# One hybrid decoder layer in fp32: the order and pacing of background weight sums, and the order of seven Strassen products

## The chip, the cores and the metric

The kernel runs on one core of one Trainium2 chip. The metric is the time of the whole program on the device, in microseconds; before the change it is 2766.74, the median of three runs from 2760.09 to 2771.63. The core has five engines that run side by side and wait for each other through semaphores: TensorE (PE in the profile) multiplies matrices into PSUM, VectorE (DVE) and ScalarE (ACT) do elementwise work, GpSimd (POOL) does elementwise work and issues some transfers, SyncE (SP) issues most of them. Transfers run on 16 DMA engines that all queues share.

## The reference, cut to what matters

One layer of a decoder is computed for 2048 prompt tokens and 64 sample tokens (8 sequences of 8), all in fp32:

```python
h = rms_norm(x, norm_mix_pre[l])
proj = h @ w_in                                   # 1024 x 3080
q, k, v, z, xbc, dt_raw, b_gate, c_gate, u_c = split(proj)
# A: three dilated attention branches, merged;  B: Mamba-2 scan;  C: gated short convolution
out = concatenate([o_a, y_b, y_c], axis=-1) @ w_out
x = x + rms_norm(out, norm_mix_post[l])
h = rms_norm(x, norm_mlp_pre[l])
f = square(relu(h @ w_mlp_up[l])) @ w_mlp_down[l]  # 1024 x 4096, 4096 x 1024
x = x + rms_norm(f, norm_mlp_post[l])
```

Keys, values and recurrent states are outputs too, so the projections store K and V as they are made.

## The kernel before, in words

**Products.** Every large fp32 product is three products of split parts: an operand is a rounded part `hi` (ScalarE) and a rest `lo` (VectorE or GpSimd), and `mm3` adds hi x lo, hi x hi and lo x hi in one PSUM bank. So each weight tile is loaded (`wraw`), split into `whi` and `wlo`, and used.

**The first part** (`front`) goes over four blocks of 512 prompt tokens. `in_qkv(B)` makes K, V and Q of a block and stores them: K and Q in the three layouts of the branches, K and V rows to the outputs as well, through the tiles `kt` and `vt`, which share three buffers with the tag `s1`. `in_rest(B)` makes everything else of the block (convolutions, scan, gates). The order is `in_qkv(b0)`, `in_rest(b0)`, then `in_qkv` of b3, b2 and b1 in a row, then `in_rest` of b1, b2, b3. The normalised and transposed input of b3 and of b2 is written to memory after it is built (`spill`, 16 transfers of 256 KB a block) and read back for `in_rest`. Attention and scan run beside this as streams. Then comes the output projection (`out_proj`), with the attention of the sample tokens as a stream, then the MLP.

**The MLP** goes over three blocks of 704 tokens. Each of its two products is a Strassen product in Winograd's form: seven products of half size instead of eight. The seven are numbered; `UP_ORDER` and `DOWN_ORDER` say in which order they run. Each is eight steps (`steps`); `w_load` loads the weights of the step four ahead, `w_split` splits the next. The left operands of the second product are formed from the tiles `x[1,1]`, `x[1,2]`, `x[2,1]`, `x[2,2]` in `down_form`; the results go to `y(t, d)` in `down_out`: token half t, column half d. In the second product the splits of weights run on VectorE, in the first on GpSimd. `end_tile` follows `down_out` with the sums of squares of finished quarters, and for products 5 and 6 two of the three token tiles are put off by a step (`late`). `next_block` loads and transposes the next block's inputs as a stream; its tiles share buffers with `x[2,2]`.

**The weight sums.** The products 5, 6, 7 and 4 take combinations of the four quarters of a weight matrix, w1 to w4 in `wsum` (product 5 takes w1, 6 takes w2, 7 takes w3, 4 takes w4). They are formed in memory by transfers alone, as a background task (`weight_sums`, kept in `behind`). A sum of a piece is a copy (kind "c") issued by SP and an accumulating transfer (kind "a") issued by GpSimd: w1 = b11 + b12 and w3 = b12 + b22 are made together in the kinds "c13" and "a13" (two transfers each), w2 = w1 + b22 in "c2" and "a2", w4 = w2 + b21 in "c4" and "a4". Each of the two matrices (u and d) is cut into 16 pieces, so there are 192 groups and 256 transfers of 256 KB. Each transfer is tied behind the last instruction of its engine with `issue_after`.

**What sets the order.** The program is written as generators. `TimedPE` counts matmul columns, 2400 a microsecond for split parts and a quarter of that for plain fp32, into `PE.us`. `poll` advances a stream when `PE.us` passes its due time, and takes the next group of sums when `behind[1]` is passed; each group moves that by `SUM_US`. If a group is still missing when `w_load` loads the first weight of a product that needs it, the loop there issues all groups up to it at once; `SUM_END` names the last kind that each product needs. The framework then orders each engine's instructions by this priority and its own estimate of when they are ready, allots buffers, and adds the semaphores.

The 192 groups are ordered by a loop over pieces in which each piece passes through the six kinds one round after the other, matrix u's pieces before d's:

```python
for s in range(len(at) + 5):
    for k, kind in enumerate(("c13", "a13", "c2", "a2", "c4", "a4")):
        if 0 <= s - k < len(at):
            group(kind, s - k)
```

Of the kernel before, what the change touches and what calls it, by code (L numbers as in the profile page):

```python
# [43 lines left out]
HT = 352  # L44
BT = 2 * HT
NSUM = 16
SUM_US = 6.4
SUM_END = {5: "a13", 7: "a13", 6: "a2", 4: "a4"}
NSP = 14

# [94 lines left out]
def hybrid_layer(ctx: ExitStack, tc: tile.TileContext, I, O, stage=9):  # L145
# [110 lines left out]
    def poll():  # L256
        for st in list(streams):
            if PE.us >= st[1]:
                advance(st)
        if behind and PE.us >= behind[1]:  # L260
            sums_on()

    behind = []
    formed = []

    def sums_on():
# [1006 lines left out]
    def weight_sums():  # L1273


        at = [(m, i) for m in "ud" for i in range(NSUM)]

        def transfer(eng, out, x, **kw):
            with tc.issue_after(eng.last):
                eng.dma_start(out, x, **kw)  # L1280

        def group(kind, piece):
            m, i = at[piece]
            n = wsum[m][0].shape[0] // NSUM
            r = slice(n * i, n * i + n)
            (b11, b12), (b21, b22) = corners[m]
            w1, w2, w3, w4 = wsum[m]
            out, src = {"c13": ((w1, w3), (b11, b12)), "a13": ((w1, w3), (b12, b22)), "c2": ((w2,), (w1,)),
                        "a2": ((w2,), (b22,)), "c4": ((w4,), (w2,)), "a4": ((w4,), (b21,))}[kind]
            for o, x in zip(out, src):  # L1290
                if kind[0] == "c":
                    transfer(SP, o[r], x[r])
                else:
                    transfer(G, o[r], x[r], accum_op=ALU.add)

        for s in range(len(at) + 5):
            for k, kind in enumerate(("c13", "a13", "c2", "a2", "c4", "a4")):
                if 0 <= s - k < len(at):
                    group(kind, s - k)
                    formed.append((kind, *at[s - k]))  # L1300
                    yield SUM_US

    corners = {}
    for m, w in (("u", I["w_mlp_up"][0]), ("d", I["w_mlp_down"][0])):
# [7 lines left out]
    def front():  # L1312
        rows = b0.prep()
        next(rows)
        next(rows)
        SP.dma_start(cst, I["c_main"])
        next(rows)
        load_gain(psT)
        next(rows)
        load_ahead(1)  # L1320
        next(rows)
        load_ahead(3)
        for _ in b0.build():
            pass
        load_vectors(psT)
        load_heads()
        SP.dma_start(abt, I["c_att"])
        load_prev()
        stream(side())
        behind.extend((weight_sums(), PE.us + 30.0))  # L1330
        yield from in_qkv(b0)
        negate_heads()
        stream(ssd_head(b0))
        def then(a, b, build=True):
            a.early = (lambda: stream(b.prep())) if build else (lambda: None)
            a.before_pair = lambda: stream(b.build() if build else b.reload())

        then(b0, b3)
        yield from in_rest(b0)
        b3.spill()  # L1340
        then(b3, b2)
        yield from in_qkv(b3)
        b2.spill()
        then(b2, b1)
        yield from in_qkv(b2)
        yield from in_qkv(b1)
        stream(ssd_head(b1))
        then(b1, b2, False)
        yield from in_rest(b1)
        stream(ssd_head(b2))  # L1350
        then(b2, b3, False)
        yield from in_rest(b2)
        stream(ssd_head(b3))
        b3.early = lambda: stream(transition())
        b3.before_pair = lambda: None
        yield from in_rest(b3)
# [209 lines left out]

    NJ = FF // P // 2
    TP = [(0, P), (P, P), (2 * P, HT - 2 * P)]
    UP_ORDER, DOWN_ORDER = (1, 2, 6, 7, 5, 3, 4), (1, 2, 7, 4, 5, 6, 3)
    e4 = s4 = w4 = r4 = v4 = f4 = y4 = t4 = psD = None  # L1570
    shifts = [(nm, src, b) for b in range(NB) for nm, src in (("s_k", "cache_attn_k"), ("s_v", "cache_attn_v"))]
    steps = [(kind, b, i, jj) for b in range(TT // BT) for kind, order in (("u", UP_ORDER), ("d", DOWN_ORDER))
# [214 lines left out]
    def down_out(i, p, ps):  # L1787
        n = TP[p][1]
        ps = ps[:n]

        def y(t, d, new=False):
            if new:
                Y[t, p] = y4.tile([P, D], F32, name=f"y{t}", tag="y")
            return Y[t, p][:n, 512 * (d - 1):512 * d]

        if i == 1:
            A.copy(y(1, 2, True), ps)
        elif i == 2:
            V.tensor_add(y(1, 1), ps, y(1, 2))
        elif i == 7:  # L1800
            V.tensor_add(y(2, 2, True), ps, y(1, 2))
        elif i == 4:
            V.tensor_add(y(2, 1), ps, y(2, 2))
        elif i == 5:
            for d in ((2, 2), (1, 2)):
                V.tensor_sub(y(*d), y(*d), ps)
        elif i == 6:
            for d in ((2, 1), (2, 2), (1, 2)):
                V.tensor_add(y(*d), ps, y(*d))
        else:  # L1810
            V.tensor_add(y(1, 2), ps, y(1, 2))
# [28 lines left out]

    def end_tile(i, p, ps):
        down_out(i, p, ps)
        for t, d in {2: [(1, 1)], 6: [(2, 1), (2, 2)]}.get(i, []):
            square(t, p, d)

    def half(b, t):
# [27 lines left out]
    for at, (kind, b, i, jj) in enumerate(steps):  # L1874
# [56 lines left out]
        if kind == "d":  # L1931
# [8 lines left out]
            if i == 3 and end:  # L1940
# [3 lines left out]
                for p in range(len(TP)):  # L1944
                    if last:
                        finish(p)
                    else:
                        late.append(lambda p=p, f=finish: f(p))
        if kind == "d" and i == 5 and jj == 4 and b + 1 < TT // BT:
            stream(next_block(b + 1))  # L1950
        if at % 20 == 10 and shifts:
            nm, sr, sb_ = shifts.pop(0)
# [42 lines left out]
```

## Time and profile before

| | |
|---|---|
| median of three runs | 2766.74 us |
| the profiled execution | 2772.1 us, its span 2770.3 us |
| TensorE busy | 2583.0 us, 93% of the span |
| VectorE, ScalarE, GpSimd busy | 1533.3, 1327.3, 1085.4 us |
| mean granted TensorE clock | 0.971 |
| moved by the DMA engines | 528.26 MB, mean 191 GB/s |

A row of the stage table gives the busy time of each engine in a stretch, the granted TensorE clock as a part of full speed, the mean busy share of the 16 DMA engines, and what they moved. A row of the waits names who waited for whom, how long in total, how often, and the longest. Line 137 is the helper through which the instructions of all engines but TensorE pass, so groups are told apart by the names of tiles. Weight loads (PEld) overlap with matmuls. In a row of one tile's instructions, the three times are the shortest, the median and the longest, in ns; then come the first and the last start.

### The profile page before, as it was taken

How to read it: one execution, taken by the hardware profiler on the slowest of the kernel's cores; microseconds unless marked ns; L12 is line 12 of the kernel's file. 1: busy time of each engine (PE TensorE's matmuls, PEld its weight loads, DVE VectorE, ACT ScalarE, POOL GpSimd, SP SyncE). 2: the span in 40 equal slices, each digit the busy share in tenths (PEclk: the TensorE clock that was granted, in tenths of full speed). 3: DMA queues.
4: the chain of work that ended last, by engine and by line, in shares of the span. 5: the costliest groups of instructions: out<-in, count | busy, mean ns of one | idle time of the engine just before them, and what ended most of it. 6: DMA issues, size and time to landing. Idle time of an engine off the chain costs nothing. (4 is left out here: it accounts for less than half of the span.)

```text
span 2770.3 us, 40697 instructions
## 1 busy us (share of the span) xinstructions
PE 2583.0 (93%) x14329; PEld 2183.1 (79%) x14329; DVE 1533.3 (55%) x2994; ACT 1327.3 (48%) x2776; POOL 1085.4 (39%) x1008
## 2 busy tenths in 40 slices
PE   7899888999999987999899999989999999999997
PEld 6898767877877865656799977779997779998775
DVE  4555536455466366555145456865446685454676
ACT  4444334435435433334455744545664455375444
POOL 4445435354354444334567500056620016661002
PEclk9999899999999988999999999999999999999999
DMA  7767998768677549878787555475434456543454
GB/s 211 210 175 221 276 245 246 199 186 225 188 205 208 156 126 290 263 234 281 210 244 207 172 162 171 139 216 169 167 129 152 135 165 205 172 167 119 130 156 95
DMA packets 426260, 528.26 MB, mean 191 GB/s; under 512 B 65482, under 2 KB 326130, under 8 KB 421448
## 3 DMA queue, kind: packets, MB, share of 16 engines
q1 hardware_dynamic: 411352, 483.45, 55.0%
q0 software_dynamic: 14704, 42.21, 9.3%
q8 instruction: 113, 1.85, 0.3%
q14 instruction: 91, 0.75, 0.1%
HBM read 447.90 MB, written 178.19 MB: 226 GB/s over the span
## 5 line engine op out<-in xcount | busy, mean ns | idle before, releaser
L137 POOL TENSOR_TENSOR wlo<-wraw,whi 128x512 fp32r<-128x512 f32 (+2 forms) x359 | 672.8, 1902 | 534.9 <-ACT whi L137 488.5
L137 ACT CAST whi<-wraw 128x1024 fp32r<-128x1024 f32 (+2 forms) x528 | 468.9, 892 | 410.0 <-PE pm L118 262.9
L118 PE MATMUL pm<-slo,whi 128*128 128x352 f32 x1344 | 437.3, 327 | 11.7 <-ACT whi L137 6.4
L118 PE MATMUL pm<-shi,wlo 128*128 128x352 f32 x1344 | 433.2, 328 | 6.9 <-POOL wlo L137 6.9
L118 PE MATMUL pm<-shi,whi 128*128 128x352 f32 x1344 | 438.7, 326 | 0.0
L118 PE MATMUL pm<-wlo,shi 128*128 128x512 f32 (+1 forms) x1008 | 398.3, 395 | 1.8 <-ACT shi L137 1.7
L118 PE MATMUL pm<-whi,shi 128*128 128x512 f32 (+1 forms) x1008 | 396.2, 393 | 0.0
L118 PE MATMUL pm<-whi,slo 128*128 128x512 f32 (+1 forms) x1008 | 336.5, 398 | 3.5 <-DVE slo L137 3.2
L137 DVE TENSOR_TENSOR wlo<-wraw,whi 128x1024 fp32r<-128x1024 f32 (+1 forms) x169 | 206.1, 1220 | 190.6 <-ACT whi L137 180.3
L118 PE MATMUL pj<-lo,whi 128*128 128x512 f32 (+1 forms) x720 | 274.8, 382 | 17.8 <-ACT xr L137 9.8
L118 PEld LDWEIGHTS pm<-slo,whi 128*128 128x128 f32 x1344 | 256.5, 191 | 14.5 <-ACT whi L137 7.7
L118 PE MATMUL pj<-hi,whi 128*128 128x512 f32 (+1 forms) x720 | 264.5, 367 | 0.0
L118 PE MATMUL pj<-hi,wlo 128*128 128x512 f32 (+1 forms) x720 | 263.8, 367 | 0.0
L118 PEld LDWEIGHTS pm<-shi,wlo 128*128 128x128 f32 x1344 | 254.9, 191 | 8.9 <-POOL wlo L137 8.8
L137 POOL TENSOR_TENSOR ssf<-ssf 128x1 f32<-128x1 f32 (+1 forms) x18 | 14.0, 775 | 627.1 <-ACT jkf L137 627.0
L118 PEld LDWEIGHTS pm<-shi,whi 128*128 128x128 f32 x1344 | 256.5, 191 | 0.2
L137 DVE TENSOR_TENSOR x<-pm,x 128x352 f32<-128x352 f32 x240 | 123.5, 521 | 227.9 <-PE pm L118 227.7
L118 PEld LDWEIGHTS pm<-wlo,shi 128*128 128x128 f32 (+1 forms) x1008 | 181.0, 180 | 60.8 <-ACT shi L137 11.0
L118 PEld LDWEIGHTS pm<-whi,slo 128*128 128x128 f32 (+1 forms) x1008 | 177.0, 179 | 61.0 <-DVE slo L137 14.3
L118 PEld LDWEIGHTS pm<-whi,shi 128*128 128x128 f32 (+1 forms) x1008 | 180.6, 179 | 49.6
L137 ACT CAST shi<-x 128x352 fp32r<-128x352 f32 x288 | 137.1, 484 | 158.7 <-DVE x L137 105.4
L137 ACT ACTIVATE x<-x 128x352 f32<-128x352 f32 x384 | 183.3, 495 | 43.9 <-DVE x L137 39.3
(322 smaller groups left out, 4744.6 us busy)
## 6 DMA issues: line engine op xcount, KB each, us to landing
wraw<-in_w_in SPq DMA_DIRECT2D x192, 256.0 KB
wraw<-u_d SPq DMA_DIRECT2D x96, 512.0 KB
wraw<-d_d SPq DMA_DIRECT2D x96, 512.0 KB
wraw<-in_w_mlp_up SPq DMA_DIRECT2D x72, 512.0 KB
wraw<-in_w_mlp_down SPq DMA_DIRECT2D x72, 512.0 KB
u_d<-in_w_mlp_up POOLq DMA_DIRECT2D x64, 256.0 KB, 5.8
d_d<-in_w_mlp_down POOLq DMA_DIRECT2D x64, 256.0 KB, 6.9
out_s_k<-in_cache_attn_k SPq DMA_DIRECT2D x8, 2040.0 KB
```

Of the source, the lines that this page charges most:

```text
L118: return self.eng.matmul(out, lhsT, rhs, **kw)
L137: out = f(*args, **kw)
```

## The change

The 192 groups take another order: matrix u before d, and in each the kinds "13", then "2", then "4", over all 16 pieces; the accumulate of a piece follows two pieces behind its copy. No group is issued while the three projections `in_qkv(b3)`, `in_qkv(b2)` and `in_qkv(b1)` are written out (`hold`); after them the due time is set to the present. The step between groups is 6.6 instead of 6.4.

In the second MLP product, the order of the seven products is 1, 2, 7, 5, 6, 4, 3 instead of 1, 2, 7, 4, 5, 6, 3. Product 5 first copies `y(2,2)` to `y(2,1)` on ScalarE, product 4 adds to `y(2,1)`, and the sum of squares of `y(2,1)` is taken after product 4. The stream of the next block starts at step 6 of product 6 (the fifth in the new order), where it started at step 4 of product 5 (the fifth in the old).

```diff
-SUM_US = 6.4
+SUM_US = 6.6
...
-        if behind and PE.us >= behind[1]:
+        if behind and not hold[0] and PE.us >= behind[1]:
             sums_on()
...
-        for s in range(len(at) + 5):
-            for k, kind in enumerate(("c13", "a13", "c2", "a2", "c4", "a4")):
-                if 0 <= s - k < len(at):
-                    group(kind, s - k)
-                    formed.append((kind, *at[s - k]))
-                    yield SUM_US
+        todo = [(k, p) for m in range(2) for w in ("13", "2", "4") for i in range(NSUM + 2)
+                for k, p in (("c" + w, i), ("a" + w, i - 2)) if 0 <= p < NSUM for p in [NSUM * m + p]]
+        for kind, piece in todo:
+            group(kind, piece)
+            formed.append((kind, *at[piece]))
+            yield SUM_US
...
+        hold[0] = True
         yield from in_qkv(b3)
         b2.spill()
         then(b2, b1)
         yield from in_qkv(b2)
         yield from in_qkv(b1)
+        hold[0] = False
+        behind[1] = PE.us
...
-    UP_ORDER, DOWN_ORDER = (1, 2, 6, 7, 5, 3, 4), (1, 2, 7, 4, 5, 6, 3)
+    UP_ORDER, DOWN_ORDER = (1, 2, 6, 7, 5, 3, 4), (1, 2, 7, 5, 6, 4, 3)
...
         elif i == 4:
-            V.tensor_add(y(2, 1), ps, y(2, 2))
+            V.tensor_add(y(2, 1), ps, y(2, 1))
         elif i == 5:
+            A.copy(y(2, 1), y(2, 2))
             for d in ((2, 2), (1, 2)):
                 V.tensor_sub(y(*d), y(*d), ps)
...
-        for t, d in {2: [(1, 1)], 6: [(2, 1), (2, 2)]}.get(i, []):
+        for t, d in {2: [(1, 1)], 6: [(2, 2)], 4: [(2, 1)]}.get(i, []):
             square(t, p, d)
...
-        if kind == "d" and i == 5 and jj == 4 and b + 1 < TT // BT:
+        if kind == "d" and i == 6 and jj == 6 and b + 1 < TT // BT:
             stream(next_block(b + 1))
```

More of the change, by code (lines that the diff above doesn't have):

```diff
@@ L259, in poll @@
                 advance(st)
-        if behind and PE.us >= behind[1]:
+        if behind and not hold[0] and PE.us >= behind[1]:
             sums_on()
     behind = []
+    hold = [False]
     formed = []
```

## The prediction

> **What bounds the kernel now.** I read the page first, then the busy times by stage, then, for the stage that stands out, the waits, the DMA queues and the transfers of the weight sums. The page says that TensorE sets the time, 93% busy over the whole span. What can be won is its remaining 187 us of idle time and the clock lost around it, so the question is where that lies.
>
> ```profile
> span 2770.3 us, 40697 instructions
> PE 2583.0 (93%) x14329; PEld 2183.1 (79%) x14329; DVE 1533.3 (55%) x2994; ACT 1327.3 (48%) x2776; POOL 1085.4 (39%) x1008
> ```
>
> The busy times by stage (columns: stretch in us, its length, busy time of each engine, granted clock, DMA share, GB/s). The rows are block 0's second projection part, the three pure attention projections (247 to 436), the other three second parts, the output projection, the first block's up product, its down product, and the next block's up product.
>
> ```profile
> 80.00:247.00 167.00, 156.06 (x1176) 148.79 (x1175) 98.37 (x239) 74.06 (x198) 82.88 (x99) 0.98 0.68 179
> 247.00:436.00 189.00, 160.27 (x914) 132.57 (x913) 80.88 (x171) 67.69 (x134) 87.48 (x94) 0.90 0.96 273
> 436.00:1036.00 600.00, 549.62 (x3235) 458.88 (x3233) 323.28 (x809) 266.82 (x724) 273.15 (x313) 0.96 0.68 189
> 1036.00:1306.00 270.00, 237.92 (x1273) 157.45 (x1274) 152.40 (x392) 103.35 (x298) 105.06 (x166) 0.94 0.88 269
> 1306.00:1576.00 270.00, 260.70 (x1526) 246.09 (x1525) 110.98 (x192) 153.05 (x288) 174.05 (x108) 0.98 0.73 216
> 1576.00:1820.00 244.00, 241.88 (x1062) 184.44 (x1061) 166.34 (x261) 122.48 (x207) 10.50 (x14) 1.00 0.51 161
> 1820.00:2046.00 226.00, 219.41 (x1344) 218.24 (x1343) 116.80 (x168) 135.12 (x235) 141.61 (x67) 0.98 0.51 163
> ```
>
> The projections at 247 to 436 have the highest DMA share (0.96) and the lowest clock (0.90); TensorE idles 189 - 160.3 = 28.7 us there. From 1306 on it idles little. The idle share runs with the DMA share: 8.4% at 0.68 (436 to 1036), 11.9% at 0.88, 15.2% at 0.96.
>
> Who ends those idle times (waits from 247 to 436: TensorE's rows, then ScalarE's), and the three instructions behind the longest:
>
> ```profile
> PE pk L118 <- DVE dtall L137: 14.7, 3, 8.5
> PE pj L118 <- DVE dtall L137: 6.2, 1, 6.2
> PE pkt L122 <- DVE yn L137: 4.1, 1, 4.1
> PE pkt L122 <- ACT kt L137: 3.3, 1, 3.3
> ...
> ACT kt L137 <- DMA out_p_k<-kt: 24.7, 5, 9.5
> ```
>
> ```profile
> 288.48 0.59 PE L118 MATMUL pk<-wlo,hi 128*128 128x264 f32 x1 [5.21 <-DVE dtall L137]
> ...
> 357.29 0.59 PE L118 MATMUL pk<-wlo,hi 128*128 128x264 f32 x1 [8.53 <-DVE dtall L137]
> ...
> 420.84 0.77 PE L118 MATMUL pj<-lo,whi 128*128 128x512 f32 x1 [6.20 <-DVE dtall L137]
> ```
>
> `kt` and `vt` share three buffers (tag s1). Each must be stored (`out_p_k`, `out_p_v`, `v_d`) before it is written again, and the PSUM bank of the V product stays full until `vt` and `dtall` have read it. So a late store holds ScalarE and VectorE, then TensorE. The stores are late because the DMA engines are full:
>
> ```profile
> q1 hardware_dynamic: 72935, 47.73, 84.3%
> q0 software_dynamic: 672, 3.67, 11.5%
> ...
> L137 POOL DMA_DIRECT2D u_d<-in_w_mlp_up x15: 757/822/1192, 251.4 to 434.2; - x15
> L137 SPq DMA_DIRECT2D u_d<-in_w_mlp_up x10: 504/542/586, 250.6 to 422.3; - x10
> L137 SPq DMA_DIRECT2D u_d<-u_d x6: 480/480/527, 286.0 to 427.2; - x6
> ```
>
> (Packets, MB, share of the 16 engines from 247 to 436; then the sums' transfers: count, issue time in ns, first and last start.) The 15 accumulates, 256 KB each, are nearly all of queue 0: 11.5% of 189 is 21.7 us, 1.45 us each. The 16 copies are 4.19 of queue 1's 47.73 MB; 4.19/47.73 of 84.3% of 189 is 14.0 us, 0.87 each. A mean transfer is 1.16 us of all 16 engines. Without them the stage's demand falls from 182 to 146 us (to 153 if only the 25 leave that the pacing counts below; the window's edges take in six of its neighbours').
>
> **What moves where.** The pacing clock counts matmul columns over 2400 a microsecond (fp32 four times), so where each group falls follows from the code alone. The three projections advance it by about 122, of which 93 are their own products (per block 4 tiles x 24 x 512 plus 96 x 264 columns): 19 groups, 25 transfers at a step of 6.4. These leave. With 122 more of delay, 192 steps of 0.2 more, and two transfers for each "13" group, the counts from before to after, worked out by stage: block 0's second part 33 to 42, the three other second parts 89 to 75, the output projection 62 to 76, the first up product 38 to 30, its down product 5 to 29. The total stays 256, and so do the matmuls and the bytes. The sums now end 160 later on that clock, at about step 40 of the first down product; the last eight groups aren't due when the first weight of product 4 is loaded (four steps ahead of step 40), so the loop in `w_load` issues them at once there.
>
> **The terms**, in us, minus for faster:
>
> 1. The three projections. Two readings. By the row of shares: 146 us of demand in some 172 is 0.85, where the stages around 0.88 idle 11.4%, so 28.7 falls to about 21, and the clock rises from 0.90 to about 0.945, 5% of 160: together -15. By the waits: the long stalls are 4.1 + 3.3 + 5.2, 8.5 and 0.9 + 6.2; the transfers issued from the start or the stall before up to each are
>
> ```profile
> L137 POOL DMA_DIRECT2D u_d<-in_w_mlp_up x4: 822/890/995, 251.4 to 285.2; - x4
> L137 SPq DMA_DIRECT2D u_d<-in_w_mlp_up x2: 505/546/586, 250.6 to 251.2; - x2
> L137 SPq DMA_DIRECT2D u_d<-u_d x1: 481/481/481, 286.0 to 286.0; - x1
> ...
> L137 POOL DMA_DIRECT2D u_d<-in_w_mlp_up x6: 772/875/1192, 303.5 to 346.5; - x6
> L137 SPq DMA_DIRECT2D u_d<-in_w_mlp_up x3: 504/536/585, 301.7 to 356.2; - x3
> L137 SPq DMA_DIRECT2D u_d<-u_d x2: 480/504/527, 303.0 to 337.4; - x2
> ```
>
> 8.4 us of engine time before the first and 13.0 before the second, so the first would keep 4 us and the other two vanish: -24, and -7 for the slow clock just behind them. I take -19, nearer to the first reading, because spills and loads of 256 and 512 KB fill the engines in bursts without any sum. Bounds -5 and -31.
>
> 2. Block 0's second part: 9 transfers more are 10 us, a share of 0.74; on the line from 0.68 to 0.88 that is 1.1% of 167: +2. Bounds 0 and +5.
>
> 3. The other second parts: 14 fewer, share down 0.03, 0.5% of 600: -3. Bounds -6 and 0.
>
> 4. The output projection: 14 more are 16 us, a share of 0.94; on the line from 0.88 to 0.96 it would idle 2.5% more of 270, +7, and +13 with the clock. But its idle time is ended by DMAs in few places:
>
> ```profile
> PE pt L122 <- DVE ct L137: 6.1, 1, 6.1
> PE pt L122 <- DVE clo L137: 6.0, 6, 2.3
> ...
> PE pkk L122 <- DMA kn<-in_cache_attn_k: 2.5, 3, 1.6
> PE pos L118 <- DMA vn<-in_cache_attn_v: 2.4, 4, 1.1
> ```
>
> I take +5. Bounds 0 and +13. The Trainium skill, DMA: Bandwidth & Descriptors, Issuing engines are not separate DMA queues, says that transfers from every issuing engine run on the same 16 DMA engines and interleave. Read strictly, this speaks against the change: work is moved, not removed, and a stage that is nearly full pays for all of it, so +16 here and a sum of -2. The rows of the two queues bear the sharing out (84.3% and 11.5% make the 0.96); whether the stage pays, they can't say.
>
> 5. The first block's MLP. The up product idles for other reasons: 0. In the down product 24 more transfers take the share from 0.51 to 0.62, on a POOL that is busy 10.5 of 244 us, and TensorE idles 2.1 us: +1, which holds the eight groups issued at once. Weight loads run four steps ahead (a step is 244/56 = 4.4 us). If the load of product 4 had to wait for the last of eight accumulates, cover is gone: +10, the upper bound; 0 the lower.
>
> 6. The order of the second product. Added: nine copies of 128x512 on ScalarE; the nearest row is the eviction in the same stage. VectorE's subtraction of `y(2,2)` waits for it, and behind that stand its next splits, which run a step ahead.
>
> ```profile
> L137 ACT COPY y<-pm 128x512 f32<-128x512 f32 (+1 forms) x3 | 1.8, 586 | 0.5 <-PE pm L118 0.4
> L137 DVE TENSOR_TENSOR y<-pm,y 128x512 f32<-128x512 f32 (+1 forms) x18 | 11.5, 682 | 1.3 <-PE pm L118 1.3
> ...
> L122 PE MATMUL pq<-cst,xt x36: 244/272/302, 1713.3 to 1751.3; 128*128 128x128 f32 x24, 96*128 96x96 f32 x12
> ...
> 1715.00:1820.00 105.00, 103.24 (x457) 77.59 (x456) 84.42 (x140) 56.10 (x98) 9.69 (x13) 1.00 0.59 191
> ```
>
> 9 x 0.586 = 5.3 us of ScalarE, busy half of the stage: hidden; 5.3 if not. Product 4's three additions and squares now stand right before product 3, undeferred. The next block's rows and transposes need the buffers of tile (2,2), which product 4 reads, so their end moves from 1751 to about 1785, 35 us before the next up product. VectorE is 80% busy in the last 105 us, and product 4 forms no difference on it (saving 16 x 0.52 = 8 us there), so this fits. +1 for two block changes; bounds -3 and +10.
>
> Sum: -19 + 2 - 3 + 5 + 1 + 1 = -13. The profiled execution took 2772.1 us (1.8 around its span), 5.4 over the runs' median of 2766.74. So 2759 there, **2754 as a median**.
>
> **Rivals.** (a) Full recovery: the stalls have no cause but the sums, and the later stages absorb them: -31 + 2 - 3 + 0 + 1 = -31, 2736. For it: 35 us of stall and lost clock in a stage whose demand falls by a fifth. Against: queue 1 keeps 146 us. (b) No recovery: three buffers and the bursts of spills make the stalls, sums or none; -5 + 2 - 3 + 5 + 2 = +1, 2768. For it, the slice of the first stall, whose share stands above 1 with only five of the sums issued since 250:
>
> ```profile
> 270.00:280.00 10.00, 5.06 (x36) 4.00 (x34) 1.63 (x3) 2.15 (x7) 4.38 (x9) 0.84 1.04 383
> ```
>
> (c) Slower: the accumulate catches up with its own copy. It was issued seven groups behind it (45 on the pacing clock), now three (20, some 22 us). POOL waits in order, and its splits of `wlo` for TensorE, norms and stores' inputs stand behind. What one such wait costs at the shortest distance is on record:
>
> ```profile
> POOL d_d L137 <- DMA d_d<-d_d: 20.2, 1, 20.2
> ...
> DMA to landing us min/median/max: 4.6/8.5/14.0
> ```
>
> The second row, the sums' accumulates in the output projection, shows landings up to 14 us from POOL's queue; the copies wait longer on SP's. If a third of the 66 accumulate groups before the MLP waited 3 us, POOL would lose 66 us, and with half of it past the four weight tiles of lead the price is +33: 2787. It decides from 27 us passed on. Against: the splits have slack, POOL is under half busy in every stage before the MLP.
>
> **How the numbers follow.** Forecast 0.46, own range 2742 to 2766; (a) 0.19, 2727 to 2742; (b) 0.17, 2762 to 2776; (c) 0.18, 2776 to 2800. A tenth left out on either side makes 2730 to 2784. About 0.5% is what a measurement of this kernel can tell from no change, that is 2753 and 2781. Faster: all of (a) and half of the forecast, 0.42. Slower: most of (c) and a little for term 4 at its bound, 0.19. Same: 0.39.
>
> **What would show it.** No `u_d` transfer between about 255 and the start of block 1's second part; the share of these projections near 0.85, their idle time near 15 us, the clock at 0.94 or more; ScalarE's wait for `out_p_k` under 12 us. The output projection at a share of 0.94 and at most 5 us longer. The last `d_d` accumulates near 1735, all at once, with no idle time of TensorE behind them; the up products' starts unmoved against their down products. It is wrong if the projections keep their stalls with the sums gone (b), if POOL waits for `u_d` copies by tens of us (c), or if the output projection grows by ten.

## The result and the profile after

The changed kernel takes 2747.44 us (median of five runs, 2745.07 to 2754.54) where the kernel before takes 2766.74 (median of five, 2760.09 to 2771.63). The ratio is 0.9925, with a 95% interval from 0.9908 to 0.9942: faster by 0.75%, and by more than 0.5% over the whole interval. The forecast was 2754, so the gain is 19 us where 13 were predicted.

The first two lines of the page after:

```profile
span 2752.8 us, 40740 instructions
PE 2578.7 (94%) x14329; PEld 2179.7 (79%) x14329; DVE 1510.2 (55%) x2994; ACT 1332.3 (48%) x2785; POOL 1086.8 (39%) x1008
```

This profiled execution is the longest of the five runs (2754.54 us), as the profiled one of before also lay 5 us over its median; their spans differ by 17.5 us.

The prediction's stage table used round times. To compare two kernels, each stage has to begin and end at the same instruction, so the rows below are cut at marks found in each trace: the first three rows are block 0's second part, the three pure projections (from the last eviction of the second K of block 3 to the last Q eviction of block 1) and the other second parts up to the first product with `w_out`; then the output projection, the same together with the first up product, and the first down product. The busy times by stage of before, between these marks (stretch in us, length, busy times, granted clock, DMA share, GB/s):

```profile
77.40:267.70 190.30, 179.23 (x1321) 169.38 (x1320) 108.67 (x255) 85.65 (x223) 95.67 (x114) 0.98 0.71 192
267.70:435.00 167.30, 138.71 (x784) 113.80 (x784) 71.93 (x153) 55.89 (x111) 76.87 (x80) 0.89 0.96 272
435.00:1002.20 567.20, 520.21 (x3110) 437.10 (x3109) 310.36 (x786) 256.10 (x696) 263.16 (x300) 0.96 0.70 194
1002.20:1345.50 343.30, 307.16 (x1579) 206.91 (x1579) 182.68 (x453) 130.37 (x372) 135.84 (x204) 0.94 0.79 241
1002.20:1576.30 574.10, 529.33 (x2930) 426.40 (x2931) 277.46 (x612) 268.38 (x615) 289.40 (x287) 0.96 0.78 234
1576.30:1819.60 243.30, 241.18 (x1057) 183.76 (x1056) 165.64 (x260) 121.78 (x206) 10.50 (x14) 1.00 0.51 161
```

The same rows of the changed kernel:

```profile
78.30:270.90 192.60, 182.66 (x1332) 171.96 (x1331) 110.11 (x255) 85.71 (x223) 98.76 (x117) 0.97 0.77 210
270.90:420.70 149.80, 135.13 (x786) 111.92 (x786) 68.94 (x148) 55.94 (x112) 67.81 (x68) 0.94 0.89 254
420.70:989.60 568.90, 524.15 (x3109) 441.88 (x3107) 310.44 (x792) 255.93 (x696) 258.88 (x296) 0.95 0.68 187
989.60:1328.70 339.10, 305.02 (x1580) 205.00 (x1579) 169.82 (x453) 130.36 (x372) 138.99 (x210) 0.94 0.85 256
989.60:1557.90 568.30, 524.23 (x2931) 422.31 (x2930) 265.27 (x612) 268.68 (x614) 288.89 (x288) 0.96 0.79 240
1557.90:1803.00 245.10, 242.02 (x1058) 183.84 (x1057) 165.59 (x260) 123.57 (x209) 20.66 (x26) 1.00 0.61 185
```

Stage by stage, after minus before: +2.3, **-17.5** in the projections, +1.7, -4.2 in the output projection, -1.6 in the up product (229.2 against 230.8, each the difference of two rows), +1.8 in the down product. What precedes 77.4 adds 0.9 and what follows the down product takes 0.9 off (949.8 against 950.7). The sum is the 17.5 by which the spans differ.

In the projections the DMA share fell from 0.96 to 0.89, the clock rose from 0.89 to 0.94, and TensorE's idle time fell from 167.3 - 138.7 = 28.6 to 149.8 - 135.1 = 14.7 us. The transfers of the up sums in a window that reaches some 20 us over the stage's start (250 to 421):

```profile
L137 POOL DMA_DIRECT2D u_d<-in_w_mlp_up x2: 857/943/1029, 251.2 to 251.8; - x2
L137 SPq DMA_DIRECT2D u_d<-in_w_mlp_up x2: 534/566/599, 403.5 to 405.2; - x2
L137 SPq DMA_DIRECT2D u_d<-u_d x1: 510/510/510, 385.8 to 385.8; - x1
```

None is issued between 252 and 385. The last three start ahead of the stage's end, although the program writes their groups behind the third projection; they are plain copies on SP's queue. The waits of TensorE, and the wait of ScalarE for its stores, in the same stretch:

```profile
PE pk L118 <- DVE dtall L137: 11.2, 2, 6.7
...
ACT kt L137 <- DMA out_p_k<-kt: 17.9, 5, 5.3
```

Of the three long stalls of before two are left, with 11.2 us in place of 14.7 + 6.2, and the wait for `out_p_k` fell only from 24.7 to 17.9. So the wait is the one that the prediction named, but it does not go away with the sums.

In the first down product, GpSimd's wait and one of its rows in order of time (start, duration, what ended the idle time before it), then TensorE's waits:

```profile
POOL d_d L137 <- DMA d_d<-d_d: 154.5, 11, 16.9
```

```profile
1714.98 2.50 POOL L137 DMA_DIRECT2D d_d<-in_w_mlp_down  x3 [12.62 <-DMA d_d<-d_d]
```

```profile
PE pm L118 <- ACT shi L137: 1.1, 3, 0.6
PE pm L118 <- DVE wlo L137: 1.1, 1, 1.1
PE pq L122 <- DMA xt<-xn_d: 0.5, 1, 0.5
```

GpSimd stood 154.5 of 245 us before accumulates, the last three of which were issued together at 1715. TensorE waited 2.7 us in all, for other things. The next block's transposes in the same product:

```profile
L122 PE MATMUL pq<-cst,xt x36: 246/271/302, 1732.2 to 1763.1; 128*128 128x128 f32 x24, 96*128 96x96 f32 x12
```

They end 205 us into the product where they ended 175 into it (1751.3 - 1576.3), 40 us ahead of the next up product at 1803.

### The profile page after: what moved, and what is told of

Same layout as the page of the kernel before. It is cut to its first block, busy times and chain, and to the rows that moved or that the text cites. A ratio compares the mean times of both kernels' runs of the same rounds, so it can differ in the third digit from the quotient of the medians.

```text
span 2752.8 us, 40740 instructions
## 1 busy us (share of the span) xinstructions
PE 2578.7 (94%) x14329; PEld 2179.7 (79%) x14329; DVE 1510.2 (55%) x2994; ACT 1332.3 (48%) x2785; POOL 1086.8 (39%) x1008
## 5 line engine op out<-in xcount | busy, mean ns | idle before, releaser
L118 PEld LDWEIGHTS pm<-whi,slo 128*128 128x128 f32 (+1 forms) x1008 | 178.3, 179 | 62.1 <-DVE slo L137 12.5
```

What stands on the lines that cost most here:

```text
L118: return self.eng.matmul(out, lhsT, rhs, **kw)
```

## The experiments

The theory was the prediction's: the sums keep the DMA engines full in the projections, three buffers pass that on to TensorE, and the pause takes it away; what the sums then cost elsewhere goes with the DMA share of the stage. The rivals: the stalls come from the spills and the short ring of buffers, sums or none (b); they come from the sums alone (a); or the gain is owed to another part of the change, the new order of the groups or of the products. Ratios are to the kernel before in runs on the same chip.

### One part alone, and no sums at all

Three kernels each have one part less or one part alone. The changed kernel without the pause:

```diff
-        hold[0] = True
         yield from in_qkv(b3)
...
-        hold[0] = False
-        behind[1] = PE.us
```

> The changed kernel without the pause: new order of the sums, step 6.6, new product order. Theory (the pause frees the DMA engines in the three pure projections): the projections take some 165 us again instead of 150, and the whole is within 0.4% of the kernel before (2757 to 2772). Rival (the order of the sums or of the products makes the gain): at least two thirds of it stay, 2747 to 2754, with the projections still near 167.

The kernel before with these three lines (and the test of `hold` in `poll`), with its old order of groups, its step of 6.4 and its old order of products:

> The kernel before with the pause alone: old order of sums and of products, step 6.4. By the code's own clock two groups are then missing when product 7 of the first down product is loaded and eleven when product 4 is, and they are issued at once. Theory: the projections still shrink by 14 to 18 us; if the groups issued at once cost nothing, the whole gains 12 to 18 (2749 to 2755); if the weight loads wait for them, TensorE idles up to 15 us in the first down product and the whole gains 0 to 8. Rival (order makes the gain): projections unchanged.

The kernel before with the new order of the products alone:

```diff
-    UP_ORDER, DOWN_ORDER = (1, 2, 6, 7, 5, 3, 4), (1, 2, 7, 4, 5, 6, 3)
+    UP_ORDER, DOWN_ORDER = (1, 2, 6, 7, 5, 3, 4), (1, 2, 7, 5, 6, 4, 3)
...
+            A.copy(y(2, 1), y(2, 2))
```

> The kernel before with the new order of the second product alone. Theory: each down product 1 to 2 us longer, each up product of blocks 2 and 3 up to 3 us shorter, the whole within 5 us of before (2762 to 2772), no change in the projections. Rival (the product order makes part of the gain): 2755 or less.

And the kernel before without any transfer of the sums; the four products that used them read as many bytes of plain quarters of the weights, so the MLP's result is of other weights:

```diff
-                    5: wsum[m][0], 6: wsum[m][1], 7: wsum[m][2], 4: wsum[m][3]} for m in "ud"}
+                    5: corners[m][0][0], 6: corners[m][1][0], 7: corners[m][1][1], 4: corners[m][0][1]} for m in "ud"}
...
-        behind.extend((weight_sums(), PE.us + 30.0))
```

> The kernel before with no weight sums at all: the four products that take them read plain quarters of the weights instead, so the second half of the layer is computed from other weights; every product, split and load of a weight stays, 256 transfers go. It bounds what any pacing of the sums can win. Theory: the projections shrink by 15 to 20, the rest of the first part and the output projection by 15 to 30 together, the MLP by under 3: 2715 to 2738. If only the projections are hurt by sums, 2745 to 2752.

Measured:

| kernel | median us | ratio to before, interval |
|---|---|---|
| before, on this chip | 2769.88 | 1 |
| change without the pause | 2776.54 | 1.0033, 1.0021 to 1.0044 |
| pause alone | 2763.68 | 0.9980, 0.9966 to 0.9993 |
| new order of products alone | 2771.29 | 0.9995, 0.9979 to 1.0010 |
| no sums | 2705.54 | 0.9772, 0.9755 to 0.9788 |

The stage rows of the kernel without the pause (the projections, the output projection):

```profile
268.90:443.70 174.80, 138.24 (x786) 113.99 (x786) 65.95 (x152) 56.12 (x112) 77.42 (x83) 0.87 0.93 257
...
1003.70:1357.00 353.30, 309.60 (x1581) 207.59 (x1580) 175.64 (x453) 130.62 (x372) 137.98 (x206) 0.93 0.78 240
```

Those of the pause alone:

```profile
264.70:420.60 155.90, 135.64 (x786) 111.56 (x786) 69.16 (x151) 55.84 (x112) 67.99 (x68) 0.93 0.88 254
...
984.40:1330.80 346.40, 306.06 (x1580) 204.89 (x1579) 180.31 (x453) 129.99 (x372) 133.72 (x202) 0.95 0.77 238
```

Of the product order alone, the projections and the first down product:

```profile
264.30:428.00 163.70, 136.48 (x784) 112.39 (x783) 70.65 (x153) 55.61 (x112) 76.62 (x80) 0.91 0.97 276
...
1564.00:1809.40 245.40, 242.07 (x1057) 183.75 (x1056) 165.61 (x260) 123.50 (x209) 10.80 (x14) 1.00 0.50 160
```

And of the kernel without sums, the first five stages, then TensorE's longest wait in its projections:

```profile
76.30:258.50 182.20, 178.49 (x1332) 169.01 (x1331) 104.17 (x255) 86.31 (x224) 85.57 (x97) 0.99 0.55 158
258.50:408.20 149.70, 134.37 (x786) 111.37 (x785) 70.19 (x150) 55.92 (x112) 68.52 (x68) 0.94 0.86 247
408.20:951.10 542.90, 511.03 (x3108) 429.47 (x3107) 307.46 (x791) 255.99 (x697) 230.54 (x256) 0.97 0.56 161
951.10:1284.90 333.80, 305.19 (x1579) 205.75 (x1579) 178.95 (x451) 130.32 (x371) 107.78 (x171) 0.94 0.63 201
951.10:1510.80 559.70, 522.84 (x2930) 421.27 (x2930) 277.56 (x610) 268.87 (x613) 245.53 (x232) 0.97 0.60 192
```

```profile
PE pk L118 <- DVE dtall L137: 11.7, 2, 7.0
```

Three things follow. The projections take 149.7 us with no sums anywhere, and 149.8 in the changed kernel: the pause recovers all that the sums cost there, to within 3 us in later traces. And the 15 us of idle time that stay (149.7 - 134.4), with two waits for `dtall` of 11.7 us, need no sums. So (a) is refuted, since part of the stalls has another cause, and (b) is refuted as to its price. Second, the projections are long without the pause (164 to 175) and short with it (150 to 156), whatever the orders. Third, the pause alone wins only 0.20% in time, which its upper end leaves at 0.07%, and the change without the pause (new order and step of the groups, new order of the products) loses 0.33%: the 0.75% of the whole is not the sum of the two.

Three of these runs missed what was expected of them. The change without the pause was slower than its range (2776.54 for 2757 to 2772), and its projections longer (174.8 for some 165). The pause alone won 6 us where 12 to 18 were expected if the groups issued at once cost nothing; its first down product took 243.3 us, as before, so the rest is not lost there, and these traces don't show where it is. And the kernel without sums was faster than its range (2705.54 for 2715 to 2738): the second parts and the output projection gave 42 us instead of 15 to 30.

### The parts in pairs, the change again, and sums put later

The changed kernel once more, unaltered, on another chip:

> The changed kernel once more, beside its parts on one chip, for a second trace: 2744 to 2754, 0.7 to 0.8% below the kernel before. The projections at 150 us again if that is the place of the gain; more than 156 in this trace would say that the first trace flattered them.

The pause and the new order of the products, with the old order and step of the groups:

> The changed kernel with the old order of the sums and their old step: pause and new product order. By the code's own clock, two groups are issued at once for product 7 of the first down product, four for product 5 and the rest for 6 and 4 later. The pause alone gained only 0.2%. If its loss lay in groups issued at once under product 4, this gains most of the whole change: 2748 to 2756. If the order of the sums matters by itself beside the pause (fewer transfers in later parts), it stays at 2758 to 2766.

The changed kernel with the old order of the products:

> The changed kernel with the old order of the second product: pause and new order of the sums. 17 groups are missing when product 4 is loaded as the fourth and are issued at once. If weight loads wait for them, TensorE idles 5 to 20 us in the first down product: 2752 to 2768, and the new product order is there to prevent it. If they don't wait, it is as fast as the whole change or 3 to 5 us faster (no copies on ScalarE, no longer down products): 2742 to 2750.

And the changed kernel with a wider step for matrix u and a narrow one for d, so that more of the sums fall into the MLP, where they had cost little:

```diff
-SUM_US = 6.6
+SUM_US = 8.6
+D_SUM_US = 2.9
...
-            yield SUM_US
+            yield SUM_US if at[piece][0] == "u" else D_SUM_US
```

> The changed kernel with other steps: 8.6 for the first matrix and 2.9 for the second, whose 96 groups then run in the first block's MLP. Without any sums the kernel took 2705.5, of which the changed kernel's 2747 has 42 still to win, nearly all before the MLP. Theory (sums cost where the DMA engines are over two thirds busy, nearly nothing in the MLP): 2722 to 2738. Rival (POOL, which issues the accumulates and splits weights in the up product, becomes the bound there): first up product 10 to 30 us longer, 2740 to 2765.

| kernel | median us | ratio to before, interval |
|---|---|---|
| before, on this chip | 2768.18 | 1 |
| changed kernel again | 2746.29 | 0.9922, 0.9910 to 0.9935 |
| pause and product order | 2771.98 | 1.0011, 0.9999 to 1.0022 |
| changed, old order of products | 2747.48 | 0.9930, 0.9917 to 0.9943 |
| changed, later sums | 2751.73 | 0.9945, 0.9931 to 0.9960 |

The stage rows of the changed kernel's second trace (projections, other second parts, output projection):

```profile
268.20:420.50 152.30, 135.96 (x786) 112.59 (x786) 68.34 (x147) 56.24 (x112) 68.20 (x68) 0.93 0.86 250
420.50:986.50 566.00, 519.09 (x3108) 436.08 (x3107) 307.11 (x793) 255.53 (x696) 259.93 (x296) 0.95 0.68 188
986.50:1322.90 336.40, 302.11 (x1579) 203.83 (x1579) 166.30 (x451) 130.32 (x372) 139.82 (x210) 0.95 0.85 258
```

The projections of the pause with the product order:

```profile
265.90:418.90 153.00, 134.88 (x786) 111.41 (x785) 69.05 (x150) 55.95 (x113) 68.52 (x68) 0.93 0.89 259
```

The change repeats (0.9922 beside 0.9925).

How far one trace of a stage can be trusted is seen where the program is the same. Up to the end of the output projection the kernel with the new order of products alone has on every engine the same instructions in the same order as the kernel before. So do the changed kernel with the old order of products and the changed kernel, and so do the pause with the product order and the pause alone. The rows that follow are, in this order: the output projection of the product order alone; the projections and the output projection of the changed kernel with the old order of products; and the other second parts of the pause alone and of the pause with the product order.

```profile
992.70:1335.10 342.40, 307.22 (x1578) 207.14 (x1579) 182.22 (x453) 130.39 (x372) 135.87 (x204) 0.94 0.78 242
...
267.10:418.30 151.20, 136.34 (x786) 113.09 (x786) 67.97 (x147) 56.12 (x113) 67.61 (x68) 0.93 0.87 251
...
986.80:1326.00 339.20, 303.27 (x1579) 203.83 (x1579) 169.18 (x453) 130.37 (x372) 139.70 (x210) 0.95 0.85 256
...
420.60:984.40 563.80, 520.79 (x3109) 437.40 (x3107) 307.63 (x788) 255.84 (x696) 264.95 (x301) 0.95 0.71 195
...
418.90:994.10 575.20, 531.52 (x3108) 446.18 (x3107) 309.02 (x789) 255.86 (x696) 265.89 (x301) 0.93 0.69 191
```

With the same instructions the projections took 167.3 and 163.7 us before the change, and 149.8, 152.3 and 151.2 after it; the output projection 343.3 and 342.4 before, and 339.1, 336.4 and 339.2 after. These repeat within 4 us. The difference in the projections is far larger, and the output projection is shorter after the change in every pair of traces, by 3 to 7 us. But the other second parts took 563.8 and 575.2 with the same instructions, so a single trace can be 11 us off in a stage.

The new order of the products neither wins nor loses in two of three comparisons: 0.9995 alone, and 0.9922 with it beside 0.9930 without it in the changed kernel. In the third, the pause with it has 1.0011 and without it 0.9980, with intervals that don't meet. These two ran on different chips, and part of what their traces differ by lies in the second parts, where their instructions are the same. So what makes that difference is open.

It isn't needed against a stall either. With the old order the loop in `w_load` has to issue more groups at once, and the first down product of that kernel shows no loss, though GpSimd waits there too:

```profile
1555.50:1799.20 243.70, 241.56 (x1059) 183.76 (x1058) 165.78 (x260) 122.21 (x207) 20.42 (x26) 1.00 0.61 186
```

```profile
POOL d_d L137 <- DMA d_d<-d_d: 87.1, 8, 16.6
```

The pause with the product order missed both of its ranges (2771.98, above 2766). What the pause wins in its projections (153.0, 14 us less than before) is gone in its total (1.0011). Its trace has the difference in the second parts (575.2, 8 more than before) and the output projection (347.9, 5 more), but the pause alone has the same instructions there and took 563.8 and 346.4. So the 5 us are seen twice, and the 8 us are not.

The later sums missed their expectation of 2722 to 2738. Their output projection and first up product:

```profile
982.60:1324.90 342.30, 302.60 (x1580) 205.20 (x1580) 177.06 (x451) 129.94 (x372) 132.65 (x202) 0.94 0.79 241
1324.90:1559.60 234.70, 220.47 (x1353) 218.42 (x1352) 100.59 (x159) 138.58 (x242) 168.57 (x102) 0.97 0.90 258
```

The output projection had 64 transfers instead of 77 and a share of 0.79 instead of 0.85, and was not shorter than in the changed kernel (342.3 against 339.1 and 336.4). The up product had 76 instead of 32 and took 234.7 us instead of 229.2; without sums it took 225.9 (559.7 - 333.8). That is 0.12 us a transfer at one in 3 us, and 0.10 at one in 7: a small price at either pace, but not nothing. This trace is of the longest of its six runs, 9 us over the median, so where the rest of the expected gain stayed can't be read from it.

### A fourth store buffer, and the old step

By the prediction, the ring of three buffers is the link between the stores and TensorE. Both kernels with a fourth, in all five places of the tag:

```diff
-            vt = epool.tile([P, 256], F32, name="vt", tag="s1", bufs=3)
+            vt = epool.tile([P, 256], F32, name="vt", tag="s1", bufs=4)
```

> The changed kernel with four buffers for K and V rows (tag s1) where it had three. Without any sums the projections still idle some 15 us, 11 of them on the V product behind VectorE, which waits for stores. Theory (a buffer comes free only when its store has landed, eight uses a block): the projections go from 150 to 140 to 146 us, the whole to 2738 to 2745. If the stall were the burst of spills itself, whatever the buffers, they stay at 149 to 152 and the whole within 4 us of the changed kernel.

> The kernel before with four such buffers instead of three, sums and all. Theory (sums delay stores, stores hold the three buffers): the projections shrink from 165 to 155 to 160 with the sums still in them, the whole to 2756 to 2764. If the buffers aren't the link between the sums and TensorE, 163 to 168 and no change of the whole.

And the changed kernel with the old step:

```diff
-SUM_US = 6.6
+SUM_US = 6.4
```

> The changed kernel with the step of 6.4 of the kernel before. The stages' counts change by two or three transfers each, so on the price of some 0.25 us each nothing is to be seen: 2743 to 2752. A result more than 6 us away would say that the order of instructions that the framework works out anew with each edit moves the time by as much as the parts told apart here outside the projections.

| kernel | median us | ratio to before, interval |
|---|---|---|
| before, on this chip | 2769.38 | 1 |
| changed, four buffers | 2742.93 | 0.9901, 0.9876 to 0.9926 |
| before, four buffers | 2764.22 | 0.9982, 0.9965 to 0.9999 |
| changed, step 6.4 | 2764.41 | 0.9976, 0.9962 to 0.9990 |

The projections of the changed kernel with four buffers, and its longest wait for `dtall` there:

```profile
266.50:410.60 144.10, 137.74 (x801) 113.77 (x800) 67.06 (x157) 56.13 (x112) 66.32 (x67) 0.96 0.91 263
```

```profile
PE pk L118 <- DVE dtall L137: 2.3, 2, 2.1
```

The projections of before with four buffers:

```profile
262.40:423.40 161.00, 140.84 (x787) 116.59 (x786) 64.31 (x144) 54.90 (x109) 72.80 (x77) 0.89 0.97 268
```

With the sums gone, the fourth buffer takes most of the rest: idle 144.1 - 137.7 = 6.4 us instead of 14.7, the wait for `dtall` 2.3 instead of 11.2. With the sums there it takes a fifth to a third of what the pause takes (161.0 against 163.7 and 167.3, the pause 149.8). So the ring passes the late stores on, but with the engines at 0.97 a longer ring doesn't make up for them. The changed kernel with four buffers has the lowest median of all, 2742.93; its interval overlaps that of the changed kernel, so that it beats the kernel before is shown, and that it beats the change is not. The kernel before with four buffers came out just outside what was expected (2764.22 for 2756 to 2764, projections of 161.0 for 155 to 160).

The old step missed its expectation of 2743 to 2752 by far. A step 3% smaller leaves 5 of the 19 us (2764.41 against 2769.38), with the projections as short as in the changed kernel (151.7):

```profile
273.00:424.70 151.70, 135.12 (x786) 111.78 (x785) 69.20 (x149) 55.61 (x112) 67.76 (x68) 0.93 0.88 254
...
989.40:1337.80 348.40, 309.84 (x1580) 208.24 (x1579) 178.49 (x453) 130.22 (x371) 140.67 (x210) 0.93 0.84 252
```

```profile
PE pkk L122 <- DMA kn<-in_cache_attn_k: 6.3, 3, 4.1
```

The output projection has 79 transfers where the changed kernel has 77, at a share of 0.84 where it has 0.85, and takes 9 to 12 us more. Neither the number of transfers nor the share tells these two apart. This trace is of the longest of its twelve runs, so the 9 to 12 us may be more than its median run has.

This run also bears on the order of the groups. The pause with the product order differs from it only in that order, and has 1.0011 where this has 0.9976. But the pause alone, with the old order of the groups and of the products, has 0.9980. The step of 6.6 is then worth another 0.5%. So the new order of the groups is worth something between nothing and 0.35% here, and the old order with the pause and a step of 6.6 was not run: whether the gain needs the new order is not shown.

### Half a step later

If it isn't how many transfers fall into the output projection, it may be where each falls. The changed kernel with every group after the pause due half a step later:

```diff
-        behind[1] = PE.us
+        behind[1] = PE.us + 3.3
```

> The changed kernel with the first group after the pause due half a step (3.3 on the pacing clock) later; step and counts per stage as in the changed kernel, each later group falls between other instructions. With a step of 6.4 the output projection took 348 us where the changed kernel takes 336 to 339, and the whole 17 more. If the count of transfers in a stage sets its time, this is the changed kernel again: output projection 335 to 341, 2743 to 2752. If it is where each transfer falls among the loads and the order that the framework finds around it, the output projection can land anywhere from 336 to 350 and the whole up to 2765; the projections stay at 149 to 153 in both.

It took 2755.08 us (2746.19 to 2768.09), a ratio of 0.9962, 0.9943 to 0.9981, beside 2766.38 of before on that chip: 8 us slower than the change, and a gain half as large. The projections and the output projection:

```profile
270.10:419.30 149.20, 134.58 (x786) 111.60 (x785) 70.38 (x150) 55.87 (x112) 69.09 (x68) 0.94 0.87 251
...
984.70:1327.20 342.50, 306.88 (x1578) 206.16 (x1579) 177.12 (x453) 129.83 (x372) 141.93 (x210) 0.94 0.85 253
```

Again 77 transfers and 0.85, and 342.5 where the changed kernel has 339.1, 336.4 and 339.2. By the medians, 8 of the change's 19 us hang on the phase of the groups, though the two intervals only just miss each other. Where they go this trace does not show: its output projection is 3 to 6 us longer, but its span is 2749.9, and the three traces of the changed kernel's instructions have 2752.8, 2741.8 and 2745.6.

## Why the prediction was right, and where it wasn't

**Term 1, the projections: right, -11 to -18 for -19.** Against the trace of before, three traces give -17.5, -15.0 and -16.1; against the second trace with its instructions (163.7), -13.9, -11.4 and -12.5. That is near the reading by the share (-15) and half or less of the reading by the waits (-31). What the waits' reading missed is shown by the kernel without sums: two of the three stalls stay, with a share of 0.86 and no sum anywhere. The ring of three has a part in them, since a fourth buffer takes the idle time to 6.4 us. That the spills fill the engines there is a reading; no run leaves them out.

The share's reading came to its -15 by other parts than the trace shows. It had the idle time fall by 8 us, to 21, and took 7 to 8 from the clock, as if TensorE's busy time fell by as many percent as the clock rose. The idle time fell by 13.9, to 14.7, and the busy time by 3.6 (138.7 to 135.1), with the clock up from 0.89 to 0.94. So the sum is near in part by luck. Of the signs, the clock and the idle time near 15 came out, but the share was 0.89 for 0.85 and the wait for `out_p_k` 17.9 for under 12. The forecast took out the 31 transfers of its round window; between the marks lie 26, and the prediction's other value, 153 us of demand in some 170, is 0.90.

**Terms 2 and 3, the second parts: too small to tell.** +2.3 for +2 in block 0's, but the second trace with before's instructions is 3.6 shorter there (186.7). In the others +1.7, -1.2 and +1.3 for -3, in a stage where the same instructions once differed by 11 us.

**Term 4, the output projection: wrong, and it is the step that failed.** The forecast was +5 within 0 and +13, by the idle time that goes with a DMA share. Between two traces of before's instructions and three of the change's, the stage became 3.2 to 6.9 us shorter, with the transfers up from 63 to 77 and the share from 0.79 to 0.85. The prediction's row from 1036 to 1306 is the fullest part of the stage, which between the marks runs from 1002 to 1345. The same stretch of the changed kernel, from 34 us after the stage's start:

```profile
1023.40:1293.40 270.00, 241.18 (x1282) 159.49 (x1282) 142.07 (x396) 103.67 (x298) 112.83 (x176) 0.93 0.96 287
```

The share rose there from 0.88 to 0.96, even above the 0.94 of the forecast. But TensorE's idle time fell from 32.1 to 28.8 us, where the forecast let it rise by 7 before it was cut to +5. So the step that failed is that idle time follows the share. The line was read across different stages, and the kernel without sums shows the price within this one: 63 transfers and 0.16 of share cost 343.3 - 333.8 = 9.5 us, 0.15 us a transfer, so the 14 more should have cost 2.

Around this stands a scatter that is larger. With 77 to 79 transfers the stage took 336 to 348 us, by phase and step alone, and the longest of all, 353.3 without the pause, has only 68; traces with the same instructions lie within 3 us. So in this kernel the stage's length hangs more on the placement of the transfers, and the order of instructions that comes with it, than on their number. What makes one placement better wasn't found. With step 6.4 the stage waits more for the cache's loads (6.3 us for `kn`, 1.6 in the changed kernel's trace), but without the pause it waits only 3.2 and is longer still.

The prediction set a rule beside this term: the Trainium skill, DMA: Bandwidth & Descriptors, Issuing engines are not separate DMA queues, by which transfers of all issuers run on the same 16 engines. Read strictly, as if a nearly full stage paid for all of the work moved into it, it made +16 here. The engines' share did rise with the 14 transfers, but the stage did not pay: -3.2 to -6.9.

**Term 5, the first MLP block: right.** The down product is 1.8 and 1.1 us longer for +1, and the groups issued at once cost nothing that shows, not even with the old order of products, where by the pacing clock 17 were issued at once. The last accumulates came at 1716.2, 158 us into the product; the forecast's 1735, on the time axis of before, is 159.

**Term 6, the order of products: right, nothing.** The ratio alone is 0.9995. In one trace each, the down product is 2.1 us longer (245.4 against 243.3), and from its start to the end of the program the kernel takes 1190.2 us (2754.2 - 1564.0) where before takes 1194.0 (2770.3 - 1576.3), which is within what two traces differ by. The transposes end 30 us later in the product, for 34 forecast.

**Rival (c)** described something that happens, GpSimd standing before an accumulate until its copy lands, for up to 16.9 us. Its distance was misread: the changed code puts an accumulate three groups behind its copy only at the ends of a kind, and five in between. Still, in the down product the accumulates catch up: the one at 1701.6 stood for 16.3 us and started 4.3 us after SP had issued a copy, at 1697.3. But there GpSimd stands for 154.5 us and has little else to do (busy 20.7 us). In the output projection the like of it (waits of `d_d` for other transfers) took 13.0 us, and accumulates into `u_d` never waited for a transfer in that trace. The 27 us from which the rival decides were not reached where they count.

So in the traces the forecast's -13 became -17.5: term 1 gave 1.5 less, term 3 gave 5 less, and term 4 gave 9 more, with the wrong sign. The part that every kernel with the pause has is the projections', 149 to 156 us in all of them with three buffers. The 3 to 7 us of the output projection are luck of the placement as far as these runs show, since half a step or 3% of a step takes them away and more. Why the kernels with the pause and a step of 6.4 gain between -4 and +6 us in the whole, with projections of 152 to 156, stays open.

## What to carry over

Look for the stage in which background transfers meet short rings of buffers and full DMA engines, and keep them out of it: here that stage paid 0.5 to 0.7 us a transfer and the others 0.1 to 0.3. Measure the price of background work by leaving it out once; the stage rows of that one run say more than a price by share read across stages. Look at two traces before believing a difference of one stage. In a kernel whose order comes from due times, vary the step and the phase before crediting a part of a change with a few microseconds.

## What the runs showed that was not expected

All 256 transfers together cost 2769.88 - 2705.54 = 64 us before the change, and their price differs by stage. From the rows of before and of the kernel without sums, over the transfers in each stretch: 17.6 us for 26 in the projections (0.68 each), 8.1 for 33 in block 0's second part (0.25), 24.3 for 87 in the other second parts (0.28), 9.5 for 63 in the output projection (0.15), 4.9 for 40 in the up product (0.12). With the second trace of before's instructions the first two prices are 0.54 and 0.14, and the third and fourth 0.25 and 0.14. After the change 2747.44 is still some 42 us over the kernel without sums.

A step of 6.4 instead of 6.6 costs 14 of the 19 us, and half a step of phase 8, with the same work and the same bytes. And GpSimd stood for 63% of a stage (154.5 of 245.1 us), and the stage was not more than 2 us longer than before.
